# Seven block products for the SwiGLU input product, on a normalized input, and an output projection by token quarters

## The chip, the cores and the metric

The kernel runs on one core of a Trainium2 chip. The metric is the device time of one execution in microseconds (us). A run lists one time for each of several executions, and their median counts.

## The reference

One step of a one-layer hybrid decoder, in float32, on 1024 prompt tokens and 8 decode tokens (T = 1032 columns), model width 1024. The part in front (a mixer of three sliding-window attention groups and a Mamba-2 branch) is the same in both kernels. The change begins where its two results are projected back:

```python
mix = concatenate([attn, ssm]) @ w_out          # 512 + 1024 features -> 1024
h = x + rmsnorm(mix, norm_mix_post)
hcat = rmsnorm(h, norm_ffn_pre) @ w_ffn_in      # 1024 -> 2 x 2816
gate, up = hcat[..., :2816], hcat[..., 2816:]
y = h + rmsnorm((silu(gate) * up) @ w_ffn_out, norm_ffn_post)
```

## The kernel before

Features lie on the 128 partitions and tokens in the columns. Every large product is made exact to float32 in three passes: each operand is split into a high part in float32r and the rest, and a `unit` issues, for each of its k tiles, high x high, low x high and high x low into one PSUM bank (line 169). The tokens go in three chunks of 344 columns (`CH`). Weights come in tiles of 1024 columns through two `wr` buffers; `load_w` splits them into `wh` and `wl`, two buffers each, mostly on GpSimd (lines 156 and 158).

The order of instructions on each engine is fixed when the program is built: a planner takes the ready instruction with the lowest priority number, and the block `prio(kind)` around code gives the number: "evac" comes first, then "w" (weights), "side", and "main" (the large products) last. A tile of a pool takes a slot (`bufs`) when the last reader of an earlier tile is done with it. All transfers are issued from SyncE's queue (SP). `next_copy` spreads the copies of the decode caches (88 of about 1 MB each) over the large products at `RATE` copies for each evacuated unit.

**Output projection** (lines 937 to 1040). The state-space part of the first two chunks is multiplied for all eight tiles m into `mix[m]`, then the attention part for chunk 0 and chunk 1, and, ahead of chunk 2, its state-space part. For each chunk a column sum of squares is built from `acc` and `sq` (`stat`), `finish` sums it over the partitions with a matmul of ones and takes the root and the reciprocal (`rms`, line 192), and then the chunk is normalized, the residual is added, and the result is written to DRAM (`h_d`) and split into `fh` and `fl`, scaled by the next norm's weights alone. The row scale `rf` of that norm is applied after the SwiGLU product. `fh` and `fl` take the 16 slots of the pool `act` that `sh` and `sl`, the split state-space input, held.

**SwiGLU** (lines 1042 to 1180). Hidden tiles t = 0 to 21 are taken in four groups (6, 6, 6 and 4 tiles). `ffn_in` makes for each tile and chunk a unit for the gate (`pg`) and one for the up half (`pu`), 24 matmuls of 344 columns each; VectorE and ScalarE turn them into silu(gate) x up, split into `hh` and `hl`, which stay on chip. After each group `ffn_out` multiplies its tiles with their rows of `w_ffn_out` and adds the result to `fac`. The first two tiles' last chunk is put late, so that other chunks cover its norms. The last group works in chunks of 388, 388 and 256 columns (`CL`), with its weights `ow` split ahead and the residual `hres` loaded back from `h_d`; after each chunk comes the last norm, and the output is added and stored.

## Time and profile before

| | us |
|---|---|
| median of 3 runs | 1949.28 |
| lowest and highest run | 1946.99, 1952.03 |
| the profiled execution: its span, first to last instruction (no other time of it is listed) | 1955.3 |
| TensorE matmul busy | 1827.1 (93%) |
| VectorE busy | 1071.0 (55%) |
| GpSimd busy | 856.4 (44%) |
| ScalarE busy | 549.2 (28%) |

The span is that of one profiled execution, 6.0 us above the median of the runs. Busy shares are averages over stages with different limits, so windows of single stages are read instead. PE is TensorE's matmul, PEld its weight load, DVE is VectorE, ACT is ScalarE, POOL is GpSimd, SP is SyncE; us from the span's start place a row. Matmuls are pipelined and their recorded lengths overlap, so the pace is read from their starts.

### The profile page before, as it was taken

To read this page: it belongs to the slowest core of one execution; us is meant where nothing else is said; L and a number is where in the kernel's file an instruction comes from. 1 tells how busy PE (TensorE), PEld (TensorE's weight loads), DVE (VectorE), ACT (ScalarE), POOL (GpSimd) and SP (SyncE) were. 2 spreads that over 40 slices of the span, in tenths; PEclk is the share of its full clock that TensorE was granted. 3 is DMA by queue.
4 is the path that set the end of the run, shared out by engine and by line. 5 is a ranking of instruction groups with operands and counts; after the bars stand their busy time and mean duration, and the time that the engine had idled before them with its cause. 6 is when DMAs were issued, how large, how long until landed. Compare 5 with 4: busy or idle time off the path is not lost.

```text
span 1955.3 us, 29265 instructions
## 1 busy us (share of the span) xinstructions
PE 1827.1 (93%) x11685; PEld 1712.4 (88%) x11685; DVE 1071.0 (55%) x1917; ACT 549.2 (28%) x1084; POOL 856.4 (44%) x557
## 2 busy tenths in 40 slices
PE   7999989999999999998789889999999999999994
PEld 7998777888887898886678879999999999999993
DVE  7866776768774554556884796330233223321348
ACT  5322344343533344452231334111111001100142
POOL 6332356665435534356755564223223332233325
PEclk9999999999999999999889999999999999999997
DMA  5322333443324433365554444236533753355362
GB/s 188 114 92 87 111 110 100 126 127 110 117 83 153 161 99 104 130 233 150 154 158 130 134 134 151 97 128 244 178 108 103 253 172 119 119 202 196 116 251 87
DMA packets 125545, 275.27 MB, mean 141 GB/s; under 512 B 17616, under 2 KB 83632, under 8 KB 124000
## 3 DMA queue, kind: packets, MB, share of 16 engines
q1 hardware_dynamic: 125408, 273.39, 42.8%
q8 instruction: 92, 1.51, 0.3%
q14 instruction: 45, 0.37, 0.1%
HBM read 235.86 MB, written 125.47 MB: 185 GB/s over the span
## 4 chain that ended last, share of the span: by engine, by line
PE 39%; DVE 7%; DMA 2%; issue 1%; POOL 1%; ACT 1%; DVEq 0%; SPq 0%; POOLq 0%; ACTq 0%
PE g L169 14%; PE pu L169 12%; PE pg L169 12%; DMA nt<-n_d 1%; DVE mix L1030 1%; DVE fl L1033 1%; PE g L954 1%; DVE nt L856 1%; DVE nt L855 1%; DMA xr<-in_xT 0%; DVE mix L1029 0%; POOL nt L854 0%; DVE fr L192 0%; DVE nr L192 0%; DVE sl L924 0%
## 5 line engine op out<-in xcount | busy, mean ns | idle before, releaser
L169 PE MATMUL g<-xh,wh 128*128 128x344 f32 x1344 | 446.0, 332 | 32.4 <-DVE rw L239 12.7
L169 PE MATMUL g<-xl,wh 128*128 128x344 f32 x1344 | 443.2, 330 | 2.8 <-DVE xl L218 2.7
L169 PE MATMUL g<-xh,wl 128*128 128x344 f32 x1344 | 441.9, 329 | 1.9 <-POOL wl L158 1.2
L156 POOL TENSOR_SCALAR wh<-wr 128x1024 fp32r<-128x1024 f32 (+1 forms) x133 | 140.4, 1056 | 674.5 <-PE g L169 355.8
L158 POOL TENSOR_TENSOR wl<-wr,wh 128x1024 fp32r<-128x1024 f32 (+1 forms) x133 | 312.8, 2352 | 9.8
L169 PEld LDWEIGHTS g<-xh,wh 128*128 128x128 f32 x1344 | 258.1, 192 | 46.4 <-issue 14.4
L169 PEld LDWEIGHTS g<-xh,wl 128*128 128x128 f32 x1344 | 258.1, 192 | 11.5 <-issue 7.5
L169 PEld LDWEIGHTS g<-xl,wh 128*128 128x128 f32 x1344 | 258.0, 192 | 11.0 <-issue 6.1
L239 DVE TENSOR_TENSOR u<-pu,rf 128x344 f32<-128x344 f32 x66 | 34.0, 515 | 237.5 <-PE pu L169 237.5
L169 PE MATMUL pg<-fh,wh 128*128 128x344 f32 x504 | 158.8, 323 | 4.9 <-DVE mix L1010 4.9
L169 PE MATMUL pg<-fl,wh 128*128 128x344 f32 x504 | 162.1, 322 | 0.0
L169 PE MATMUL pu<-fl,wh 128*128 128x344 f32 x504 | 161.8, 321 | 0.0
L169 PE MATMUL pg<-fh,wl 128*128 128x344 f32 x504 | 161.4, 320 | 0.0
L169 PE MATMUL pu<-fh,wh 128*128 128x344 f32 x504 | 161.0, 319 | 0.0
L169 PE MATMUL pu<-fh,wl 128*128 128x344 f32 x504 | 160.4, 318 | 0.0
L169 PE MATMUL g<-hl,wh 128*128 128x344 f32 x432 | 137.8, 319 | 0.0
L169 PE MATMUL g<-hh,wl 128*128 128x344 f32 x432 | 137.4, 318 | 0.0
L169 PE MATMUL g<-hh,wh 128*128 128x344 f32 x432 | 137.1, 320 | 0.0
L659 ACT ACTIVATE sm<-sm,ngm 128x128 f32<-128x128 f32 (+1 forms) x192 | 84.9, 443 | 183.5 <-DVE ngm L655 177.2
L1088 ACT CAST hh<-s 128x344 fp32r<-128x344 f32 x66 | 31.7, 480 | 296.6 <-DVE s L1087 296.6
L614 ACT COPY sw<-rw 32x1032 f32<-32x1032 f32 x96 | 101.0, 1052 | 30.5 <-DVE rw L239 29.4
L1085 ACT ACTIVATE s<-s 128x344 f32<-128x344 f32 x66 | 32.5, 492 | 247.6 <-DVE s L239 247.4
(325 smaller groups left out, 3815.9 us busy)
## 6 DMA issues: line engine op xcount, KB each, us to landing
out_skv<-in_cache SPq DMA_DIRECT2D x64, 1023.5 KB, 5.4
wr<-in_w_in SPq DMA_DIRECT2D x56, 512.0 KB, 3.7
wr<-in_w_fin SPq DMA_DIRECT2D x44, 512.0 KB, 3.6
out_skv<-in_cache SPq DMA_DIRECT2D x16, 1022.0 KB, 5.4
wr<-in_w_out SPq DMA_DIRECT2D x24, 512.0 KB, 4.7
wr<-in_w_fout SPq DMA_DIRECT2D x24, 384.0 KB, 3.9
e<-cs_d SPq DMA_DIRECT2D x16, 512.0 KB, 4.1
n_d<-nh SPq DMA_DIRECT2D x12, 512.0 KB, 3.6
```

What stands on the lines that cost most here:

```text
L156: nc.gpsimd.tensor_scalar(out=wh[:, :cols], in0=wr[:, :cols], scalar1=1.0, scalar2=0.0, op0=ALU.mult, op1=ALU.add)
L158: nc.gpsimd.tensor_tensor(out=wl[:, :cols], in0=wr[:, :cols], in1=wh[:, :cols], op=ALU.subtract)
L169: nc.tensor.matmul(ps, x[:, ws], y[:, c0:c1], start=(k == 0 and j == 0), stop=(k == n - 1 and j == 2))
L239: return nc.vector.tensor_tensor(out=dst, in0=ps, in1=r[:dst.shape[0], c0:c1], op=ALU.mult)
L614: nc.scalar.copy(sw[q * 32:(q + 1) * 32, 0:T], rw[s * 32:(s + 1) * 32, :])
L659: nc.scalar.activation(out=sm[:, h, :nk], in_=sm[:, h, :nk], func=AF.Exp, scale=SCALE, bias=ngm[:, g, j, i:i + 1], accum_out=den[:, g, j, ...
L855: nc.vector.tensor_tensor(out=nt[:, 0], in0=nt[:, 0], in1=nt[:, 1], op=ALU.add)
L856: nc.vector.tensor_tensor(out=nt[:, 0], in0=nt[:, 0], in1=nt[:, 2], op=ALU.add)
L954: nc.tensor.matmul(pq[m][c], ws[m][j == 1][:, k * P:(k + 1) * P], (sl if j == 2 else sh)[k][:, CH[c][0]:CH[c][1]], start=(k == 0 and j == ...
L1030: nc.vector.scalar_tensor_tensor(out=mv, in0=mv, scalar=nw(MIX_POST, m), in1=x[:, m % 2], op0=ALU.mult, op1=ALU.add)
L1085: last = nc.scalar.activation(out=s, in_=s, func=AF.Silu)
L1088: nc.scalar.copy(hh[:, c0:c1], s)
```

## The change

The tokens go in four quarters of 258 columns (`QS`) from the output projection on, and the tiles `mix[q][i]` hold one quarter and four of the eight feature tiles, 4 x 258 columns.

**Output projection.** The state-space part is made for quarters 0 to 2, then the attention part for quarters 0 and 1 together, for quarter 2, the state-space part of quarter 3 and its attention part. The attention weights are loaded and split again for each of the three attention parts (12 pairs; before 8, with two pairs kept on chip). `norms(q)` normalizes, adds the residual in the tile that held x (`xr`, three buffers, two for a quarter), writes it to `h_d`, and makes the second norm before the SwiGLU product: its reciprocal is applied to the input itself.

**SwiGLU input product.** Two token halves s, each of two quarters. The weights of gate and up of one hidden tile, and the input of one half, are each cut into 2 x 2 blocks. `x_blocks(s)` forms from the four input blocks seven combinations (b11, b21, b22, t1 to t4) in place, with five subtractions of 1032 columns, and splits each into high and low (ScalarE copies; the rest on VectorE for four, on GpSimd for three). `w_blocks(t)` does the same for the weights with four sums of 512 columns and seven splits. `ffn_in(t, s, w)` makes seven products of 4 x 3 matmuls of 258 columns, each in a PSUM bank of its own out of eight, and adds them to the two quarters of gate and up. The product silu(gate) x up goes to DRAM (`hid_d`), not to the chip's own memory.

**Output product.** It begins when all 22 hidden tiles are made. `hid_load(t)` reads a tile back through an `xr` buffer and splits it into two slots out of 28 (16 of the pool `act`, 12 of `ax`), which the x blocks held before. `ffn_out` is as before, but the weights `ow` and the residual tiles `hres` of the last group take `act` slots after those of the hidden tiles. `RATE` for the copies falls from 0.52 to 0.42 for each call of `next_copy`, of which there are two in each `ffn_in`.

The core of the diff (empty lines and removed code left out):

```diff
+QW = T // 4
+QS = [(i * QW, (i + 1) * QW) for i in range(4)]
+RATE = (0.35, 0.42)
...
+    mix = [[mixp.tile([P, 4, QW], F32, tag="mix", name=f"mix{q}{i}") for i in range(2)] for q in range(4)]
+    def mv(q, m):
+        return mix[q][m // 4][:, m % 4]
+    def ssm_ev(m, ps, a0, a1):
...
+    C3 = [(0, 388), (388, 3 * QW)]
+    pq = [[gps(cw=y - x) for x, y in C3] for m in range(2)]
...
+    def ssm_part(ms, qs, share=False):
+        for m in ms:
+            w = ssm_w(m, share)
+            for q in qs:
+                ps = gps(cw=QW)
+                unit(ps, w, sh, sl, q, QS)
+                with prio("evac"):
+                    next_copy(ssm_ev(m, ps, *QS[q]))
+    ssm_part(range(2, KT), (0, 1, 2))
...
+    def att_part(qs):
+        accs = {q: np_.tile([P, QW], F32, tag="nacc", name="nacc") for q in qs}
+        for m in range(KT):
+            if m % 2 == 0:
+                pair = load_pair(m)
+            for q in qs:
+                ps = gps(cw=QW)
+                unit(ps, [x[:, (m % 2) * 512:(m % 2 + 1) * 512] for x in pair], ahs, als, q, QS)
+                with prio("evac"):
+                    nc.vector.tensor_tensor(out=mv(q, m), in0=mv(q, m), in1=ps, op=ALU.add)
+                    stat(mv(q, m), m == 0, accs[q], nc.vector)
+        return accs
...
+    def norms(q, acc):
+        c0, c1 = QS[q]
+        with prio("evac"):
+            r = np_.tile([P, QW], F32, tag="nr", name="nr")
+            finish(acc, r)
+            acc = np_.tile([P, QW], F32, tag="nacc", name="nacc2")
+            hs = []
+            for i in range(2):
+                x = np_.tile([P, 4, QW], F32, tag="xr", name="xr", bufs=3)
+                nc.sync.dma_start(out=x, in_=a["xT"][4 * i:4 * i + 4, :, c0:c1].rearrange("k p t -> p k t"))
+                hs.append(x)
             for m in range(KT):
+                h = hs[m // 4][:, m % 4]
+                (nc.gpsimd if m % 2 else nc.vector).tensor_tensor(out=mv(q, m), in0=mv(q, m), in1=r, op=ALU.mult)
+                nc.vector.scalar_tensor_tensor(out=h, in0=mv(q, m), scalar=nw(MIX_POST, m), in1=h, op0=ALU.mult,
+                                               op1=ALU.add)
+                stat(h, m == 0, acc, nc.gpsimd)
+            r = np_.tile([P, QW], F32, tag="nr", name="nr2")
+            finish(acc, r)
+            for m in range(KT):
+                nc.vector.scalar_tensor_tensor(out=mv(q, m), in0=hs[m // 4][:, m % 4], scalar=nw(FFN_PRE, m), in1=r,
+                                               op0=ALU.mult, op1=ALU.mult)
+            for i in range(2):
+                nc.sync.dma_start(out=h_d[i][:, :, c0:c1].rearrange("k p t -> p k t"), in_=hs[i])
+    acc01 = att_part((0, 1))
+    norms(0, acc01[0])
+    norms(1, acc01[1])
+    norms(2, att_part((2,))[2])
+    ssm_part(range(KT), (3,), True)
+    norms(3, att_part((3,))[3])
...
+    ax = pool(fst, "ax", 12, side="right")
+    ex = pool(fst, "ex", 2, side="right")
+    slots = [(actp, "act")] * 16 + [(ax, "ax")] * 12
+    half = {}
+    def x_blocks(s):
+        (xa, xc), (xb, xd) = mix[2 * s], mix[2 * s + 1]
+        def split(name, x, e):
+            p, tag = slots.pop(0)
+            hi = p.tile([P, T], F32R, tag=tag, name=f"x{name}h{s}")
+            p, tag = slots.pop(0)
+            lo = p.tile([P, T], F32R, tag=tag, name=f"x{name}l{s}")
+            xf = x.rearrange("p k t -> p (k t)")
+            nc.scalar.copy(hi, xf)
+            e.tensor_tensor(out=lo, in0=xf, in1=hi, op=ALU.subtract)
+            half[s, name] = (hi, lo)
+        def sub(dst, x, y):
+            nc.vector.tensor_tensor(out=dst, in0=x, in1=y, op=ALU.subtract)
         with prio("evac"):
+            split("b11", xa, nc.vector)
+            sub(xa, xb, xa)
+            split("b21", xc, nc.gpsimd)
+            split("b22", xd, nc.gpsimd)
+            sub(xb, xd, xb)
+            sub(xd, xd, xa)
+            split("t2", xd, nc.vector)
+            split("t1", xa, nc.vector)
+            split("t3", xb, nc.gpsimd)
+            sub(xc, xc, xd)
+            split("t4", xc, nc.vector)
+    x_blocks(0)
+    x_blocks(1)
+    hid_d = [dtile(f"hid_d{t}", [P, T]) for t in range(HT)]
+    wslots = [(whp, "wh"), (wlp, "wl"), (whp, "wh"), (wlp, "wl"), (ex, "ex"), (ex, "ex")] + [(mixp, "mix")] * 8
+    nws = [0]
+    banks = [(psg, "g"), (psa, "ap"), (pss, "sp"), (pst, "ap"), (psg, "g"), (psa, "ap"), (pss, "sp"), (psn, "ap")]
...
+    def w_blocks(t):
+        res = {}
+        with prio("w"):
+            g = wrp.tile([P, 1024], F32, tag="wr", name="wg")
+            nc.sync.dma_start(out=g, in_=a["w_fin"][t])
+            u = wrp.tile([P, 1024], F32, tag="wr", name="wu")
+            nc.sync.dma_start(out=u, in_=a["w_fin"][HT + t])
+            sa = rowp.tile([P, T], F32, tag="row", name="sa")
+            sb = rowp.tile([P, T], F32, tag="row", name="sb")
+            a11, a12, a21, a22 = g[:, :512], g[:, 512:], u[:, :512], u[:, 512:]
+            s1, s2, s3, s4 = sa[:, :512], sa[:, 512:1024], sb[:, :512], sb[:, 512:1024]
+            def split(name, x):
+                p, tag = wslots[nws[0] % len(wslots)]
+                nws[0] += 1
+                w = p.tile([P, 1024 if p in (whp, wlp) else T], F32R, tag=tag, name=f"w{name}")
+                nc.scalar.copy(w[:, :512], x)
+                nc.gpsimd.tensor_tensor(out=w[:, 512:1024], in0=x, in1=w[:, :512], op=ALU.subtract)
+                res[name] = w
+            split("b11", a11)
+            nc.vector.tensor_tensor(out=s1, in0=a21, in1=a22, op=ALU.add)
+            split("b21", a12)
+            nc.vector.tensor_tensor(out=s2, in0=s1, in1=a11, op=ALU.subtract)
+            split("t2", s2)
+            split("t1", s1)
+            nc.vector.tensor_tensor(out=s3, in0=a11, in1=a21, op=ALU.subtract)
+            split("t3", s3)
+            nc.vector.tensor_tensor(out=s4, in0=a12, in1=s2, op=ALU.subtract)
+            split("b22", s4)
+            split("t4", a22)
+        return res
+    def ffn_in(t, s, w):
+        def prod(name):
+            q, tag = banks[nbk[0] % 8]
+            nbk[0] += 1
+            ps = q.tile([P, 512], F32, tag=tag, name="fb")[:, :QW]
+            wt, (hi, lo) = w[name], half[s, name]
+            with prio("main"):
+                for k in range(4):
+                    wh, wl = wt[:, k * P:(k + 1) * P], wt[:, 512 + k * P:512 + (k + 1) * P]
+                    xk = slice(k * QW, (k + 1) * QW)
+                    for j, (x, y) in enumerate(((wh, hi), (wl, hi), (wh, lo))):
+                        nc.tensor.matmul(ps, x, y[:, xk], start=(k == 0 and j == 0), stop=(k == 3 and j == 2))
+            return ps
+        p = np_.tile([P, 4, QW], F32, tag="xr", name="fp", bufs=3)
+        o_ = np_.tile([P, 4, QW], F32, tag="xr", name="fo", bufs=3)
+        p1, u2, p5, u3 = (p[:, i] for i in range(4))
+        gate, up = o_[:, 0:2], o_[:, 2:4]
+        def add(dst, x, y, e=nc.vector):
+            return e.tensor_tensor(out=dst, in0=x, in1=y, op=ALU.add)
+        b = prod("b11")
+        with prio("evac"):
+            nc.scalar.copy(p1, b)
+        b = prod("b21")
+        with prio("evac"):
+            next_copy(add(gate[:, 0], p1, b))
+        b = prod("t2")
+        with prio("evac"):
+            add(u2, p1, b)
+        b = prod("t1")
+        with prio("evac"):
+            nc.scalar.copy(p5, b)
+            add(gate[:, 1], u2, p5)
+        b = prod("t3")
+        with prio("evac"):
+            add(u3, u2, b)
+            add(up[:, 1], u3, p5)
+        b = prod("b22")
+        with prio("evac"):
+            add(gate[:, 1], gate[:, 1], b)
+            nc.scalar.activation(out=gate, in_=gate, func=AF.Silu)
+        b = prod("t4")
+        with prio("evac"):
+            next_copy(add(up[:, 0], u3, b))
+            nc.vector.tensor_tensor(out=up, in0=up, in1=gate, op=ALU.mult)
+            nc.sync.dma_start(out=hid_d[t][:, 2 * s * QW:(2 * s + 2) * QW], in_=up.rearrange("p i t -> p (i t)"))
...
+    hslots = [(actp, "act")] * 16 + [(ax, "ax")] * 12
+    nhs = [0]
+    def hid_load(t):
+        with prio("w"):
+            hr = np_.tile([P, T], F32, tag="xr", name="hr", bufs=3)
+            nc.sync.dma_start(out=hr, in_=hid_d[t])
+            res = []
+            for i in range(2):
+                p, tag = hslots[nhs[0] % 28]
+                nhs[0] += 1
+                res.append(p.tile([P, T], F32R, tag=tag, name=f"h{'hl'[i]}{t}"))
+            nc.scalar.copy(res[0], hr)
+            (nc.vector if t % 2 else nc.gpsimd).tensor_tensor(out=res[1], in0=hr, in1=res[0], op=ALU.subtract)
+        hid[t] = res
...
-                nc.sync.dma_start(out=h, in_=h_d[m])
+                nc.sync.dma_start(out=h, in_=h_d[m // 4][m % 4])
...
+    for t in range(HT):
+        w = w_blocks(t)
+        for s in range(2):
+            ffn_in(t, s, w)
+    fac = [mixp.tile([P, T], F32, tag="mix", name=f"fac{m}") for m in range(KT)]
     for gi, (t0, t1) in enumerate(groups):
-        if gi == 0:
-            # the last chunk of the first two tiles late, while its norms are under way
-            ffn_in((0, 1), [(0, 0), (0, 1), (1, 0), (1, 1), (0, 2), (1, 2)])
-        for t in range(2 if gi == 0 else t0, t1):
-            ffn_in((t,), [(t, c) for c in range(3)])
+        for t in range(t0, t1):
+            hid_load(t)
```

## Rows read from the trace of the kernel before

**Rows 1.** Windows in order: length, busy us (instructions) by engine, granted clock, DMA share, GB/s.

```profile
991.90:1069.00 77.10, 69.09 (x381) 66.53 (x382) 46.00 (x52) 11.55 (x19) 43.08 (x23) 0.90 0.48 142
1069.00:1098.00 29.00, 29.00 (x185) 28.78 (x184) 21.50 (x29) 8.96 (x15) 11.60 (x7) 1.00 0.23 72
1098.00:1172.00 74.00, 57.59 (x320) 54.26 (x320) 64.62 (x72) 27.67 (x54) 48.34 (x32) 0.93 0.51 162
1172.00:1201.00 29.00, 25.24 (x155) 24.43 (x153) 23.95 (x34) 16.27 (x28) 17.14 (x13) 0.96 0.53 180
1201.00:1877.00 676.00, 676.00 (x4291) 675.85 (x4290) 189.21 (x301) 76.57 (x157) 207.03 (x130) 1.00 0.45 153
1930.00:1955.30 25.30, 1.22 (x2) 0.50 (x2) 18.12 (x22) 2.32 (x5) 14.96 (x14) 0.55 0.30 105
```

**Rows 2.** The chain that ended last: start, length, work.

```profile
1312.05 67.74 PE g L169 x432
...
1877.56 23.36 PE g L169 x132
```

**Rows 3.** Timeline of TensorE, last output group: start, length of the merged instructions.

```profile
1919.13 0.80 PE L169 MATMUL g<-hh,ow 128*128 128x256 f32 x2 [4.15 <-DVE fac L1132]
...
1924.45 0.40 PE L169 MATMUL g<-hh,ow 128*128 128x256 f32 x2
...
1926.91 0.40 PE L169 MATMUL g<-hh,ow 128*128 128x256 f32 x2
```

**Rows 4.** Costs by line, GpSimd and ScalarE, from 990 us on: busy, mean ns.

```profile
L1119 POOL TENSOR_TENSOR ow<-wr,ow 128x512 fp32r<-128x512 f32 x8 | 11.0, 1410 | 19.7 <-ACT ow L1118 19.7
...
L979 POOL TENSOR_TENSOR wl<-wr,wh 128x1024 fp32r<-128x1024 f32 x6 | 14.5, 2424 | 15.0 <-ACT wh L978 15.0
...
L1118 ACT CAST ow<-wr 128x512 fp32r<-128x512 f32 x8 | 4.6, 617 | 3.7 <-PE pu L169 2.4 <-DMA wr<-in_w_fout 1.2
```

**Rows 5.** Costs by line on VectorE, 1069 to 1201 us.

```profile
L1033 DVE SCALAR_TENSOR_TENSOR fl<-mix,par,fh 128x344 fp32r<-128x344 f32 x24 | 23.2, 1001 | 1.1 <-ACT fh L1032 1.0
L1030 DVE SCALAR_TENSOR_TENSOR mix<-mix,par,xr 128x344 f32<-128x344 f32 x24 | 21.9, 952 | 2.2 <-DMA xr<-in_xT 2.2
L995 DVE TENSOR_TENSOR nacc<-nacc,sq 128x344 f32<-128x344 f32 x21 | 17.5, 835 | 6.7 <-ACT sq L994 5.9
L1029 DVE TENSOR_TENSOR mix<-mix,nr 128x344 f32<-128x344 f32 x12 | 13.3, 1170 | 0.1
L1010 DVE TENSOR_TENSOR mix<-mix,g 128x344 f32<-128x344 f32 x24 | 11.8, 500 | 2.9 <-PE g L169 2.9
...
L154 DVE TENSOR_TENSOR wl<-wr,wh 128x1024 fp32r<-128x1024 f32 x4 | 5.4, 1358 | 0.0
```

**Rows 6.** VectorE: costs from 990 us on, one tile's row (ns min/median/max), timeline.

```profile
L924 DVE SCALAR_TENSOR_TENSOR sl<-yg,par,sh 128x1032 fp32r<-128x1032 f32 x5 | 8.5, 1707 | 0.0
...
L1132 DVE TENSOR_TENSOR fac<-fac,g 128x256 f32<-128x256 f32 x8 | 3.2, 412 | 0.3 <-PE g L169 0.3
...
L192 DVE RECIPROCAL fr<-fr 128x256 f32<-128x256 f32 x1 | 1.8, 1753 | 1.9 <-ACT fr L191 1.9
...
L1167 DVE TENSOR_TENSOR fac<-fac,hres x5: 410/411/943, 1947.4 to 1949.8; 128x256 f32<-128x256 f32 x5
...
984.51 2.83 DVE L924 SCALAR_TENSOR_TENSOR sl<-yg,par,sh 128x1032 fp32r<-128x1032 f32 x1
...
992.11 1.28 DVE L924 SCALAR_TENSOR_TENSOR sl<-yg,par,sh 128x1032 fp32r<-128x1032 f32 x1
```

**Rows 7.** DMA issues: count, KB each, median us to landing.

```profile
wr<-in_w_fin SPq DMA_DIRECT2D x44, 512.0 KB, 3.6
...
hres<-h_d SPq DMA_DIRECT2D x8, 516.0 KB, 10.0
```

**Rows 8.** The tail: cost by line on GpSimd, and the chain.

```profile
L1161 POOL TENSOR_TENSOR fac<-fac,hres 128x388 f32<-128x388 f32 x9 | 11.4, 1293 | 0.0
...
1941.84 1.76 DVE fr L192
```

130 lines of the change are left out of this document (25 added, 105 removed).

## The prediction

> **What bounds the kernel now.** I read the windows first, cut where the engines' shares change [rows 1]. From 1201 to 1877 us TensorE is busy for all 676.00 us at full clock, while VectorE needs 189, GpSimd 207 and ScalarE 77: hidden tiles (into SwiGLU) and their output products alternate and only matmuls set the pace. Ahead of it, between 1098 and 1201, the reader is to see the reverse: VectorE is busy 64.6 of 74.0 and 24.0 of 29.0 us, TensorE only 57.6 and 25.2. That is the seam, where the output projection, two norms and the first hidden tiles meet. Behind 1930 a tail of 25.3 us has almost no matmul. So the change has three prices, each from its own stretch: matmuls in the full stretch, VectorE in the seam, transfers at the two new joints behind it.
>
> Then the pace of one matmul. The chain of waits has 432 matmuls of 344 columns in 67.74 us, 156.8 ns each [rows 2]. At 256 columns, 21 matmuls start between 1924.45 and 1926.91 us, 117.1 ns each [rows 3]; so 258 columns are 118.0 ns, and the matmul costs by column (0.456 and 0.457 ns each).
>
> **The SwiGLU product.** Before: 22 tiles x 3 chunks x 2 halves x 24 = 3168 matmuls x 156.8 = 496.7 us. After: 22 tiles x 2 token halves x 7 products x 12 = 3696 x 118.0 = 436.1 us. That is -60.6 us, or 19.8 us a tile. It holds only if nothing else needs 19.8 us. POOL splits seven 512-column blocks, 1.41 us each [rows 4]: 9.9 us, where it now has two of 1024 columns. ScalarE copies them (7 x 0.62, [rows 4]) and has six short passes, some 7 us. VectorE: ten adds from PSUM at 0.41, four between SBUF tiles and two products of 516 columns, four sums of 512: with the doubling that POOL causes (below) about 12.5 us. All are under 19.8, and eight PSUM banks let an evacuation be some 10 us late. So the saving is taken in full.
>
> A page speaks against it. In the Trainium skill, "TensorE: Matmul & The Clock Gate", section "Back-to-back issue gap", a stream of weight loads and matmuls is said to run at about 81 ns for 128 columns and 131 ns for 512. An estimate between these gives 98 ns at 258 and 109 at 344, and the product would get 17 us slower (3696 x 98 against 3168 x 109), the sum below 2016 us of span. Here the rows decide: 117 against 157 ns [rows 2, 3].
>
> **The seam.** The output projection's matmuls keep their columns (96 of 387 columns, 177 ns by column, and 1008 x 118 ns are 135.9 us, against 864 x 156.8 = 135.5), so what counts is who feeds them. State-space parts and attention for quarters 0 and 1 are 90.7 us of matmul. In the same stretch now, 106.1 us hold 566 matmuls, some 14 of them small [rows 1]: 552 x 156.8 = 86.6, so 19.5 us are lost. The same loss puts their end at 991.9 + 90.7 + 19.5 = 1102.
>
> From there VectorE has to do, before the last of the x blocks is split: the other two quarters' evacuations, 16 x 0.41 + 14 x 0.63 = 15.4 us; the norms, per quarter 4 products (0.88), 8 residuals (0.71), 8 scalings (0.75) and two reciprocals of 1.75, 18.7 us, four times 74.8; the state-space part of quarter 3, 8 x 0.41 + 4 x 1.36 = 8.7; x_blocks, 2 x 9 operations on 1032 columns at 1.70 = 30.6; first evacuations and weight sums, 7. In all 136.5 us. The prices are the means of the seam [rows 5], those of 344 columns times 258/344, and for the wide ones the scaled split of the same width [rows 6]. Now the whole seam from 1069 to 1201 has 110.1 us of VectorE work [rows 1]; x_blocks is the part that is new. It can't move forward: its tiles take the slots of sh and sl, which the state-space part of quarter 3 reads to its end, and it ends with a chain: norm, second norm, three differences, splits.
>
> The means are uncertain, and here lies the range. A two-input operation from SBUF takes 0.41 us alone and 0.94 beside one of POOL at 256 columns; at 1032 columns the rows have 1.28 and 2.83 [rows 6]. An add from PSUM stays at 0.50 [rows 5]. The Trainium skill, "SBUF — State Buffer", section "Who interferes with whom", says that a VectorE instruction with two SBUF inputs contends with a GpSimd one that reads SBUF; by that rule, which the trace bears out, x_blocks pays for its own splits on POOL. Of the 136.5 us, 94 such narrow operations (4 x 20 and 14) and 18 wide ones are 100; the rest, 36.3, is fixed. All alone, 36.3 + 94 x 0.41 + 18 x 1.28 = 98 us; all contended, 36.3 + 94 x 0.94 + 18 x 2.83 = 176. I take 130, nearer to the means: norms, weight splits and x_blocks keep POOL busy as now, but in the last 30 us it has only splits, so eight scalings and nine wide operations cost 6 us less.
>
> So the last block is ready at 1102 + 130 = 1232. By then TensorE has had all of tile 0 but the last product (1.4 us), and up to three products of tile 1 (4.2 us), whose weights find slots. The product thus behaves as if it had begun at 1232 + 1.4 - 19.8 - 4.2 = 1209.9. Before, counted back from 1877.56, it behaves as if it began at 1877.56 - 496.7 - 3 x 67.74 = 1177.7 [rows 2]. The seam costs +32 us (0 to +77 with the bounds).
>
> **Joint into the output product.** The hidden tiles come back from DRAM into three xr buffers that the last two ffn_in calls still hold. Only tile 0 can be loaded early; five loads follow, two or three at a time, each 3.6 to 10.0 us [rows 7], with a split of about 1.1 us on ScalarE and 1.36 on VectorE or 2.4 us on POOL behind it [rows 4, 5]. A wave of loads and splits takes some 7 us, and the sixth tile comes with the second, 14 us after the last product. Meanwhile the six free banks can take tile after tile, 18 matmuls or 2.8 us each. No overlap costs 12 us, full overlap 3; I take 7, with the matmuls at half clock behind a wait: the two behind the 4.15 us one took 0.80 us in place of 0.40 [rows 3].
>
> **Joint into the last group.** Its weights (ow) take act slots that group 2 reads until its end, so the first split (0.62 + 1.41 us, [rows 4]) is bare: +3 us (1 to 5). Now they are split while hidden tiles run.
>
> **The tail.** hres needs eight act slots. Now fh and fl are done with them in time; after the change tiles 18 to 21 sit there and the last unit reads them. The eight loads, 10.0 us to landing each when queued together [rows 7], move behind the last matmul, and with them 16 adds of 388 columns (nine of them on POOL, 1.29 us each, [rows 8]). The last norm's reciprocal already ends at 1943.6 [rows 8], 14 us after the last matmul, with VectorE busy 18.1 of the tail's 25.3 us [rows 1]; the adds fall in beside it and leave VectorE freer ahead of it. Nine adds on POOL, 11.6 us, from 12 us on, when hres has landed, end some 24 us behind the last matmul, and a store follows: +2 us (-4 to +12). Slower pacing (0.42 in place of 0.52) leaves some eight cache copies for the last group in place of four; they are issued ahead of hres, at nothing, and if they delay it, within that +12.
>
> **Sum.** 1955.3 - 60.6 + 32 + 7 + 3 + 2 = 1938.7 us for the span. The profiled span is 6.0 us above the median of the runs, 1949.28; the same distance gives 1933 us. A measurement here can tell 0.3%, 5.8 us, from no change.
>
> **Rivals.** (a) The seam stays hidden: VectorE's operations run as if alone, no loss, 1906.7, a time of 1901. For it: POOL is busy for only 0.65 of 1098 to 1172 us. Against it: the means, measured at that share, are 1.5 to 2 times the least values. (b) It ends slower: the seam takes the gain. That decides once VectorE's 130 us become 147 (+48.6 us, the net gain without the seam). The x_blocks splits and 12 pair splits (2.4 us) on POOL raise its share, and a contended mean half way between 136 and 175 puts the seam at +58: 1964, a time of 1958. For it: windows that are already 87% VectorE. Against it: list order puts the attention's evacuations into gaps. (c) The full stretch isn't TensorE's any more: in-order evacuations on VectorE behind contended sums cost 1 us a tile, +22 us, time 1955. For it: VectorE's share rises from 0.28 to 0.63; against: 10 us of banks. (d) The change doesn't do what it says: a matmul of 258 columns costs as 344. 3696 x 156.8 = 579.5 us, +143 against the sum, 2076. The page above points this way; the 256-column rows speak against it.
>
> **How the numbers follow.** Forecast 0.48 (its own range 1918 to 1950), (a) 0.17, (b) 0.25, (c) 0.08, (d) 0.02. The range for 8 in 10 reaches from (a) into (b): 1902 to 1967. Chances, by the same cases. Faster: 0.42 of the forecast, (a) whole, 0.01 of (c): 0.60. Within 0.3% (1943.4 to 1955.1): 0.05 and 0.04 and 0.04 of forecast, (b) and (c): 0.13. Slower: the rest, 0.27.
>
> **What would show it.** Right: seven products of 12 matmuls at 118 ns without idle time between tiles, 436 us; a VectorE busy over 0.85 from 1100 to 1230; first steady tile at about 1232; a gap under 10 us ahead of the first output unit; hres landing behind the last matmul. Wrong: waits of TensorE on POOL or VectorE inside the 22 tiles, a seam that ends before 1215 or after 1250, or a joint with a bare 15 us.

## The result, and the profile after

The kernel after takes 1972.9 us (median of four runs, 1971.74 to 1975.82), the one before 1949.65 (four runs, 1946.99 to 1952.03): a ratio of 1.0120, 95% interval 1.0105 to 1.0136. It is slower by 1.2%, where the forecast was 1933 us and its range ended at 1967. The profiled execution took 1973.6 us, with a span of 1971.8.

Windows of the kernel after, columns as in [rows 1]:

```profile
1069.00:1098.00 29.00, 28.09 (x234) 27.83 (x232) 18.81 (x31) 12.56 (x23) 11.45 (x5) 1.00 0.23 73
1098.00:1130.00 32.00, 22.54 (x149) 20.98 (x150) 26.47 (x32) 7.97 (x14) 22.03 (x19) 0.88 0.41 132
1130.00:1155.00 25.00, 19.17 (x113) 18.54 (x113) 17.34 (x25) 7.57 (x14) 17.64 (x16) 0.77 0.63 190
1155.00:1180.00 25.00, 18.77 (x114) 17.78 (x113) 22.95 (x30) 8.10 (x15) 17.16 (x8) 0.83 0.42 127
1180.00:1217.00 37.00, 13.49 (x58) 10.90 (x57) 32.19 (x31) 14.75 (x29) 27.88 (x21) 0.60 0.21 71
1217.00:1252.00 35.00, 16.27 (x76) 14.34 (x76) 29.40 (x45) 11.23 (x20) 16.56 (x15) 0.64 0.24 76
1252.00:1679.00 427.00, 426.57 (x3562) 426.53 (x3563) 230.01 (x428) 142.34 (x275) 208.40 (x148) 1.00 0.51 169
...
1930.00:1972.00 42.00, 9.50 (x69) 8.31 (x67) 29.16 (x38) 8.55 (x20) 21.81 (x20) 0.64 0.68 258
```

The full stretch is what was forecast: TensorE busy for all of 427 us at full clock (2.4 GHz), the other engines at half load. The loss is ahead of it. From 1180 to 1252 TensorE is busy for 29.8 of 72 us, at a granted clock of 0.60 to 0.64, and VectorE, the engine that was to set this stretch, has 10.4 us of idle time in it too.

The chain that ended last, its longest pieces from 1240 us on (start, length, work); it answers to [rows 2, 8]:

```profile
1252.43 427.00 PE fb L1152 x3564
1680.23 6.02 DMA hr<-hid_d
1687.44 4.15 DMA hr<-hid_d
1698.12 216.06 PE g L171 x1354
...
1928.97 7.27 DMA hres<-h_d
1937.17 2.49 DVE fr L194
```

3564 matmuls in 427.00 us are 119.8 ns each. The product thus counts 3696 x 119.8 = 442.8 us, and, ending at 1679.4, behaves as if begun at 1236.6. The first matmul of the last group stands at 1890.7 and its last one ends at 1938.3 (1877.4 and 1929.9 before). The terms, against the profile before:

| term | forecast | measured | from |
|---|---|---|---|
| SwiGLU product | -60.6 | -53.9 | 442.8 - 496.7 |
| seam | +32 | +58.9 | 1236.6 - 1177.7 |
| joint into the output product | +7 | +8.1 | 1890.7 - 1679.4 - 3 x 67.74 |
| last group | +3 | -4.9 | 47.6 - 52.5 |
| tail | +2 | +8.1 | 33.5 - 25.4 |
| sum | -16.6 | +16.3 | spans: 1971.8 - 1955.3 = 16.5 |

Four fifths of the miss (26.9 of 33.1 us of span) are the seam; it is the term that turned the sign. These positions are counted from the span's start, and the part ahead of the change, which both kernels share, was 4.7 us shorter in this profile than in that of the kernel before: its last two splits of the state-space input start at 996.34 us before (first row) and at 991.61 us after (second row).

```profile
996.34 2.48 DVE L924 SCALAR_TENSOR_TENSOR sl<-yg,par,sh 128x1032 fp32r<-128x1032 f32 x2
991.61 2.49 DVE L926 SCALAR_TENSOR_TENSOR sl<-yg,par,sh 128x1032 fp32r<-128x1032 f32 x2
```

Counted from their ends (998.82 and 994.10), the seam costs 242.5 - 178.9 = 63.6 us.

VectorE's reciprocals mark its steps: two for each norm, one row per instruction (x2: two back to back). The first row is norm 0's first, the second norm 0's second and norm 1's first, then norm 1's second, and norm 2's and 3's pairs:

```profile
1099.35 1.75 DVE L194 RECIPROCAL nr<-nr 128x258 f32<-128x258 f32 x1
...
1121.99 3.38 DVE L194 RECIPROCAL nr<-nr 128x258 f32<-128x258 f32 x2
...
1165.70 1.75 DVE L194 RECIPROCAL nr<-nr 128x258 f32<-128x258 f32 x1
...
1174.77 1.75 DVE L194 RECIPROCAL nr<-nr 128x258 f32<-128x258 f32 x1
...
1215.51 1.76 DVE L194 RECIPROCAL nr<-nr 128x258 f32<-128x258 f32 x1
...
1222.90 1.77 DVE L194 RECIPROCAL nr<-nr 128x258 f32<-128x258 f32 x1 [0.69 <-ACT nr L193]
...
1239.33 1.77 DVE L194 RECIPROCAL nr<-nr 128x258 f32<-128x258 f32 x1 [4.84 <-ACT nr L193]
```

The start at 1099 is the forecast's 1102. But norms 1 and 2 need 42 and 41 us from one reciprocal to the next, 83 of the 160 us up to the last x block (1259.8). The kernel before has such a norm too, with 41.6 us between the reciprocals of its chunk 1, but its second reciprocal (`rf`) is applied behind the product, which therefore does not wait for it:

```profile
1125.26 2.29 DVE L192 RECIPROCAL nr<-nr 128x344 f32<-128x344 f32 x1
...
1166.85 2.29 DVE L192 RECIPROCAL rf<-rf 128x344 f32<-128x344 f32 x1
```

GpSimd's timeline inside norm 2 of the kernel after shows what stands in between (L1012 are the seven adds of its second sum, L1125 splits of SwiGLU weights, L1080 one of an x block):

```profile
1190.61 1.89 POOL L1012 TENSOR_TENSOR nacc<-nacc,sq 128x258 f32<-128x258 f32 x2 [2.46 <-ACT sq L1011]
1192.45 2.54 POOL L1080 TENSOR_TENSOR xt3l<-mix,xt3h 128x1032 fp32r<-128x1032 f32 x1
1194.96 2.28 POOL L1125 TENSOR_TENSOR wt<-sa,wt 128x512 fp32r<-128x512 f32 x1
1197.18 1.73 POOL L1012 TENSOR_TENSOR nacc<-nacc,sq 128x258 f32<-128x258 f32 x1
1199.05 2.09 POOL L1125 TENSOR_TENSOR wt<-wu,wt 128x512 fp32r<-128x512 f32 x1
1202.42 1.54 POOL L1125 TENSOR_TENSOR wb<-sb,wb 128x512 fp32r<-128x512 f32 x1 [1.28 <-ACT wb L1124]
1203.92 0.73 POOL L1012 TENSOR_TENSOR nacc<-nacc,sq 128x258 f32<-128x258 f32 x1
1205.86 2.95 POOL L1125 TENSOR_TENSOR wb<-wg,wb 128x512 fp32r<-128x512 f32 x2 [1.21 <-ACT wb L1124]
1208.77 2.31 POOL L1012 TENSOR_TENSOR nacc<-nacc,sq 128x258 f32<-128x258 f32 x2
1211.27 1.48 POOL L1125 TENSOR_TENSOR wt<-sa,wt 128x512 fp32r<-128x512 f32 x1 [0.19 <-ACT wt L1124]
1212.71 0.91 POOL L1012 TENSOR_TENSOR nacc<-nacc,sq 128x258 f32<-128x258 f32 x1
```

The adds are spread over 23 us, and splits of SwiGLU weights, some of them waiting for ScalarE, stand between them. The order of GpSimd's list is not the only cause: there are two buffers for squares, and the last three squares came at 1202.25, 1206.21 and 1211.10 us, behind weight copies in ScalarE's list, though VectorE had their inputs ready at 1192.8 (with more buffers, in e17 below, they come at once). TensorE's own waits show the same from the other side (1095 to 1256 us; us in total, times, longest):

```profile
PE nps L1003 <- POOL nacc L1012: 18.2, 2, 11.2
PE fb L1152 <- ACT xt1h L1079: 7.7, 1, 7.7
```

The ones-matmul that finishes a norm waits at the head of TensorE's list, and what stands behind it waits as well. That is 18.2 of the 63.7 us in which TensorE has no matmul between 1099.35 and 1259.8 us.

### The profile page after: what moved, and what is told of

Same layout as the page of the kernel before. It is cut to its first block, busy times and chain, and to the rows that moved or that the text cites. A ratio compares the mean times of both kernels' runs of the same rounds, so it can differ in the third digit from the quotient of the medians.

```text
span 1971.8 us, 31805 instructions
## 1 busy us (share of the span) xinstructions
PE 1791.5 (91%) x12457; PEld 1673.1 (85%) x12457; DVE 1184.3 (60%) x2167; ACT 655.4 (33%) x1266; POOL 974.6 (49%) x657
## 4 chain that ended last, share of the span: by engine, by line
PE 36%; DVE 9%; DMA 3%; issue 1%; ACT 1%; POOL 1%; DVEq 0%; POOLq 0%; SPq 0%; ACTq 0%
PE fb L1152 22%; PE g L171 14%; DMA nt<-n_d 1%; DVE nacc L1012 1%; DVE mix L1048 1%; DVE xr L1042 1%; PE g L968 1%; DVE fac L1277 1%; DVE nr L194 1%; DMA hr<-hid_d 1%; DVE mix L1084 1%; DVE mix L1041 0%; DVE al L860 0%; DMA hres<-h_d 0%; ACT wh L996 0%
## 5 line engine op out<-in xcount | busy, mean ns | idle before, releaser
L158 POOL TENSOR_SCALAR wh<-wr 128x1024 fp32r<-128x1024 f32 (+1 forms) x91 | 96.7, 1062 | 322.6 <-PE g L171 298.3
L160 POOL TENSOR_TENSOR wl<-wr,wh 128x1024 fp32r<-128x1024 f32 (+1 forms) x91 | 210.9, 2317 | 6.8 <-PE fb L1152 0.8
L1125 POOL TENSOR_TENSOR wb<-wg,wb 128x512 fp32r<-128x512 f32 x44 | 58.4, 1349 | 167.6 <-ACT wb L1124 167.6
L171 PEld LDWEIGHTS g<-hh,wh 128*128 128x128 f32 x432 | 81.5, 189 | 5.4 <-ACT hh L1205 5.0
L617 POOL TENSOR_TENSOR sw<-sw,sin 128x1032 f32<-128x1032 f32 x24 | 71.4, 2975 | 21.8 <-ACT sw L616 21.8
L171 PEld LDWEIGHTS g<-hl,wh 128*128 128x128 f32 x432 | 81.1, 189 | 1.1 <-POOL hl L1206 1.1
L1161 DVE TENSOR_TENSOR fo<-fp 128x258 f32<-128x258 f32 x88 | 58.8, 668 | 38.4 <-ACT fp L1174 37.0
L171 PEld LDWEIGHTS g<-hh,wl 128*128 128x128 f32 x432 | 81.6, 189 | 0.0
L241 DVE TENSOR_TENSOR rw<-g,rin 128x344 f32<-128x344 f32 x108 | 54.7, 510 | 39.1 <-PE g L171 38.9
L653 DVE CUSTOM_DVE_ANT_0 sm<-sps,mask 128x128 f32<-128x128 f32 (+1 forms) x192 | 59.0, 345 | 27.5 <-PE ptp L668 17.3
```

The source lines that it names most:

```text
L158: nc.gpsimd.tensor_scalar(out=wh[:, :cols], in0=wr[:, :cols], scalar1=1.0, scalar2=0.0, op0=ALU.mult, op1=ALU.add)
L160: nc.gpsimd.tensor_tensor(out=wl[:, :cols], in0=wr[:, :cols], in1=wh[:, :cols], op=ALU.subtract)
L171: nc.tensor.matmul(ps, x[:, ws], y[:, c0:c1], start=(k == 0 and j == 0), stop=(k == n - 1 and j == 2))
L241: return nc.vector.tensor_tensor(out=dst, in0=ps, in1=r[:dst.shape[0], c0:c1], op=ALU.mult)
L617: nc.gpsimd.tensor_tensor(out=sw[:, 0:T], in0=sw[:, 0:T], in1=sin, op=ALU.mult)
L653: nc.vector.tensor_tensor_reduce(out=sm[:, h, :nk], in0=sps[h][:, c0:c0 + nk], in1=msk, scale=1.0, scalar=0.0, op0=ALU.add, op1=ALU.max, a ...
```

## The experiments

Ratios are to the kernel before, run on the same chip; "gain" is the difference to 1.0120 times 1949 us. The intervals are 3 to 6 us to either side and that of 1.0120 itself is 3, so a gain under 5 us is none that this can tell, and the 6 us of e7 and e14 are only just clear of it. Where a seam's length is compared below, it is counted from the end of the shared part (the last split of `sl`) to the point at which the product behaves as if begun: 242.5 us in the kernel after, 240.3 in e13, which is the same kernel up to its last store.

| run | edit | ratio | 95% interval | gain, us |
|---|---|---|---|---|
| e1 | own ring of three for the norms' x | 1.0124 | 1.0100 to 1.0148 | -1 |
| e2 | four squares, six sums | 1.0105 | 1.0081 to 1.0129 | 3 |
| e3 | sums of squares on TensorE, three squares | 1.0025 | 1.0007 to 1.0042 | 18.5 |
| e4 | second sums on VectorE | 1.0114 | 1.0092 to 1.0135 | 1 |
| e5 | order in pairs of quarters | 1.0053 | 1.0032 to 1.0074 | 13 |
| e6 | second norm left out | 0.9990 | 0.9976 to 1.0004 | 25 |
| e7 | x differences left out | 1.0087 | 1.0069 to 1.0104 | 6 |
| e8 | early residual tiles | 1.0079 | 1.0058 to 1.0100 | 8 |
| e9 | e3, e5, e8 | 0.9964 | 0.9947 to 0.9981 | 30 |
| e10 | e9, hidden tiles into row tiles | 0.9933 | 0.9916 to 0.9949 | 36 |
| e11 | e10, attention 2 and 3 together | 0.9930 | 0.9910 to 0.9951 | 37 |
| e14 | scaling in wide instructions | 1.0153 | 1.0134 to 1.0172 | -6 |
| e15 | e11, hidden tiles into row and ex | 0.9920 | 0.9901 to 0.9939 | 39 |
| e16 | e15 and e14 | 0.9935 | 0.9916 to 0.9953 | 36 |
| e17 | separate rings of squares | 1.0117 | 1.0085 to 1.0148 | 1 |
| e18 | e15, separate rings of squares | 0.9899 | 0.9884 to 0.9914 | 43 |

**Are the rings of buffers the wait? (e1, e2, e17)**

```diff
-  x = np_.tile([P, 4, QW], F32, tag="xr", name="xr", bufs=3)
+  x = nrm.tile([P, 4, QW], F32, tag="hs", name="xr", bufs=3)     # e1
+  sq = nrm.tile(..., tag="sq", bufs=4); nacc: bufs=6             # e2
+  sq = nrm.tile(..., tag="sq" if eng is nc.gpsimd else "sqa", bufs=4); nacc: bufs=6   # e17
```

> Three theories of the seam, used for all runs on it. From the first norm's first reciprocal (1098.7 us) to the last x block (1259) VectorE is busy 134 of 160 us; the forecast had 130 and no idle time. Rings: the norms queue for few buffers (two squares, two sums, three xr tiles, which the SwiGLU sums fp and fo share), and VectorE's 26 us of idle time come from that. Work: VectorE's 134 us set the end, and a wait that is taken away only lets other work move up. Queues: the sums of squares of the norms stand on GpSimd between weight splits (the third norm's seven adds took from 1190.6 to 1212.7, with less than 1 us each), and TensorE's ones-matmul behind them holds TensorE as well. This run gives the norms' x tiles a ring of three of their own; fp, fo and hr keep the old one. Rings: 6 to 12 us faster (1961 to 1967), with tile 0's first sums in VectorE before the last norm's scaling. Work and queues: within 3 us of 1973.

> Four squares in place of two and six sums in place of two. Rings: the statistics of quarter 2, whose evacuations end at 1116 but whose adds come at 1155 behind the second norm's squares, move up by some 30 us, and the time falls by 8 to 15 us (1958 to 1965). Work and queues: within 3 us of 1973.

> The squares of the attention parts (added up on VectorE) and those of the norms' second sums (added up on GpSimd) get rings of four of their own, so that the first sums of quarters 2 and 3 can't stand behind the second sums of quarters 1 and 2 for a buffer, and six sum tiles. Rings, in the form that the shared ring leaves the first sums waiting even at four buffers: 8 to 15 us faster (1956 to 1963), with the first reciprocal of quarter 2 before 1150 us. Queues (one gate behind the next: ScalarE's and GpSimd's order holds the second sums wherever the first ones stand): within 4 us, with the third norm's two reciprocals 40 us or more apart.

Not by themselves. In e1 the SwiGLU sums did move ahead (the first stands at 1188.12 in place of 1245.80), and the time stayed. In e17 quarter 2's first reciprocal came with norm 1's second, both at 1162 (1174.77 after), not before 1150, and its second one at 1201.99, 38 us later. In e17 the adds of that norm are no longer spread: with four squares the same seven adds take 10.7 us in place of 23:

```profile
1182.10 5.21 POOL L1014 TENSOR_TENSOR nacc<-nacc,sq 128x258 f32<-128x258 f32 x5 [4.15 <-ACT nacc L1009]
...
1189.89 2.86 POOL L1014 TENSOR_TENSOR nacc<-nacc,sq 128x258 f32<-128x258 f32 x2
```

ScalarE takes the root at 1195.28, and then VectorE comes to the reciprocal only at 1201.99, behind adds and x splits in its own list:

```profile
1195.78 2.58 DVE L1014 TENSOR_TENSOR nacc<-nacc,sq 128x258 f32<-128x258 f32 x1
1198.28 1.22 DVE L1082 TENSOR_TENSOR xt2l<-mix,xt2h 128x1032 fp32r<-128x1032 f32 x1
1199.42 1.22 DVE L1082 TENSOR_TENSOR xt1l<-mix,xt1h 128x1032 fp32r<-128x1032 f32 x1
1200.57 1.50 DVE L1014 TENSOR_TENSOR nacc<-nacc,sq 128x258 f32<-128x258 f32 x1
1201.99 1.75 DVE L194 RECIPROCAL nr<-nr 128x258 f32<-128x258 f32 x1
```

The seam is 242.3 us long in e1, 237.1 in e2 and 237.7 in e17: buffers are worth some 5 us of it at most. In e2 VectorE was busy 143.5 of 155.5 us between the first reciprocal and the last block, where it had 134.1 of 160.3 (idle time in the kernel after: 26.2): half of the idle time was filled, and most of what filled it was the same instructions taking longer.

**VectorE's work, GpSimd's work, or the order of the lists? (e3, e4, e7, e14)**

```diff
-  eng.tensor_tensor(out=acc, in0=acc, in1=sq, op=ALU.add)
+  nc.tensor.matmul(ps[:, :QW], onr, sq, start=(m == 0), stop=(m == KT - 1))   # e3, sq in fp32r, bufs=3
-  stat(h, m == 0, acc, nc.gpsimd)
+  stat(h, m == 0, acc, nc.vector)                                             # e4
-  nc.vector.tensor_tensor(out=dst, in0=x, in1=y, op=ALU.subtract)             # e7: sub() does nothing
-  for m in range(KT): nc.vector.scalar_tensor_tensor(out=mv(q, m), in0=h, scalar=nw(FFN_PRE, m), in1=r, ...)
+  nc.scalar.activation(out=mv(q, m), in_=h, func=AF.Copy, scale=nw(FFN_PRE, m))        # e14, behind stat
+  for i in range(2): nc.vector.tensor_tensor(out=mix[q][i], in0=mix[q][i], in1=r..., op=ALU.mult)
```

> The sums of squares leave VectorE and GpSimd: the squares are written as fp32r and TensorE adds them up in PSUM, 64 matmuls with ones of 258 columns (0.12 us each at full clock, 8 us in all) for 56 adds. That takes some 22 us from GpSimd and 15 from VectorE in this stretch. Work: 12 to 18 us faster (1955 to 1961). Queues: 15 to 25 us faster (1948 to 1958), with the third norm's two reciprocals under 25 us apart where they were 41. Rings: at most 5 us faster, since the rings of x tiles and the list order stay.

> The norms' 28 second sums move from GpSimd to VectorE, 0.43 to 0.8 us each, 12 to 22 us more for VectorE. Work: 8 to 20 us slower (1981 to 1993). Queues: 5 to 12 us faster (1961 to 1968), since no norm's end stands behind a weight split any more. Rings: within 4 us.

> The eight differences of the x blocks are left out (the blocks are split as they are): 13.0 us of VectorE, five of them ahead of the last block. Work: 8 to 14 us faster (1957 to 1963). Queues and rings: the first half's four stand beside waits anyway, so only the second half's four count, 3 to 6 us faster (1965 to 1968).

> The FFN norm's weights are multiplied in by ScalarE while the second sum is still being added up, and VectorE then scales by the row in two instructions of 1032 columns (1.23 us each alone) in place of eight of 258 (19.5 us for 32 in the kernel after). That takes 8 to 12 us of work from VectorE and 3 us from each norm's chain; ScalarE gets 32 passes of 0.42 us. Work or pair: 6 to 10 us faster (1963 to 1967). Queues: the norms' waits for the sums stay, only the last norm's 2 to 3 us count, at most 4 us faster.

Taking the adds from both engines gained 18 us, the upper end for work and the middle for queues; the third norm's reciprocals stand 21 us apart (1161.65 and 1182.75). As e3 also has a third buffer for squares, its gain is that of both. Handing GpSimd's adds to VectorE changed the time by 1 us, which neither forecast (the seam of that profile is 236.5 us long): VectorE was busy 143.3 of 155.5 us, GpSimd 82 in place of 104. Leaving out 13 us of VectorE's differences gave back 6, the queues' end. And e14 took 32 narrow products (19.5 us) off VectorE for eight wide ones (10.3 us) and was slower by 6: ScalarE went from 56 to 69 us busy between the first reciprocal and the last block, with 32 more passes in its list, and the last norm's second reciprocal came behind a longer wait (4.84 us in the kernel after):

```profile
1243.62 1.77 DVE L194 RECIPROCAL nr<-nr 128x258 f32<-128x258 f32 x1 [6.64 <-ACT nr L193]
```

So VectorE's work alone does not set the seam: less of it brought no gain in e14.

**What do the two engines cost each other? (e13)**

```diff
+  for i in range(16): v(nd[:, 0], nx[:, 0], nr_[:, 0])      # VectorE, 258 columns, alone
+  for i in range(16): g(np1[:, 0], np1[:, 0], nd[:, 0])     # GpSimd alone
+  for i in range(32): v(nd[:, 1], nx[:, 1], np1[:, 0])      # VectorE beside
+  for i in range(16): g(np2[:, 0], np2[:, 0], np1[:, 0])    # GpSimd
   ...                                                       # and 1032 columns: 8 and 8 alone, 4 alone, 8 beside 4
```

> The kernel after with a small block of its own behind the last store, so that only the block's rows count, not the time: VectorE products of 258 columns alone, GpSimd adds of 258 alone, then 32 of the one beside 16 of the other; then the same with differences of 1032 columns, 8 alone, 4 on GpSimd alone, 8 beside 4. If the two engines share one thing in turn (pair): beside GpSimd a VectorE product takes 0.8 us or more where it takes 0.47 alone, and the stretch of both is near the sum of the two alone (15 and 12 us: 23 to 27 us). If they only disturb each other at times (work): under 18 us for both.

Timeline of that block, a row for a run of like instructions (GpSimd's two stretches run on into each other, so each row holds the one alone and the one beside VectorE):

```profile
1978.14 8.22 DVE L1313 SCALAR_TENSOR_TENSOR mb<-mb,par,mb 128x258 f32<-128x258 f32 x16
1986.49 26.70 POOL L1316 TENSOR_TENSOR mb<-mb,mb 128x258 f32<-128x258 f32 x32 [16.61 <-DVE mb L1313]
1999.35 22.48 DVE L1313 SCALAR_TENSOR_TENSOR mb<-mb,par,mb 128x258 f32<-128x258 f32 x32 [12.99 <-POOL mb L1316]
...
2032.79 10.10 DVE L1330 TENSOR_TENSOR mb<-mb,mb 128x1032 f32<-128x1032 f32 x8
2042.96 23.05 POOL L1316 TENSOR_TENSOR mb<-mb,mb 128x1032 f32<-128x1032 f32 x8 [20.35 <-DVE mb L1330]
2052.66 18.25 DVE L1334 TENSOR_TENSOR mb<-mb,mb 128x1032 f32<-128x1032 f32 x8 [9.77 <-POOL mb L1316]
```

A narrow product alone takes 8.22 / 16 = 0.51 us. GpSimd's first 16 adds end at about 1999.3 (0.80 each), the other 16 at 2013.2. Of the 32 products, 16 ran beside these, from 1999.35 to 2013.5 (0.88 each), and 16 alone up to 2021.8. Beside each other the two go in step, one product and one add every 0.87 us. The whole stretch of 22.5 us lies between what the two theories gave (under 18, and 23 to 27). The wide difference takes 1.26 us alone and the wide add 2.4; together, from 2052.7 to 2066.0, four adds and four differences took 3.3 us each. The two engines thus nearly take turns on wide tiles (both together need 90% of the sum of the two alone) and do less so on narrow ones (67%). The Trainium skill, "SBUF — State Buffer", section "Who interferes with whom", calls the shared port pair an exclusive lock: the wide rows nearly agree, the narrow ones only in part. So 16 adds on GpSimd cost the 16 products beside them 5.9 us (14.1 in place of 8.2), 0.37 us an add, and the shortest such add on VectorE takes 0.36. This is a part of why e4 came out even, not the whole: VectorE's busy time there still rose by 9 us (143.3 for 134.1), and its idle time fell from 26 to 12.

**The start of the seam and the second norm (e5, e6)**

```diff
-  C3 = [(0, 388), (388, 3 * QW)];  ssm_part(range(2, KT), (0, 1, 2))
+  C3 = QS[:2];                     ssm_part(range(2, KT), (0, 1))              # e5
-  norms(2, att_part((2,))[2]);  ssm_part(range(KT), (3,), True)
+  ssm_part(range(KT), (2, 3), True);  norms(2, att_part((2,))[2])
-  stat(h, m == 0, acc, nc.gpsimd);  r = np_.tile(..., name="nr2");  finish(acc, r)   # e6
```

> Nothing but the order of the output projection changes: the state-space part of quarters 0 and 1, their attention part and norms, then the state-space part of quarters 2 and 3, and so on. 192 matmuls of 258 columns (22.7 us) move from ahead of the first norm to behind it, with as many loads and splits as now. Work (VectorE's sum with its start): the first reciprocal comes 20 to 23 us earlier, at about 1077 us, and the time falls by 12 to 20 us (1951 to 1959). Queues and rings: the norms start earlier but meet twice the weight splits and matmuls in the same queues, and the last x block moves by under 8 us, 1963 to 1971.

> The second norm is left out: the x blocks are scaled by the first norm's row in place of the second's. That removes 32 squares, 28 adds on GpSimd, four ones-matmuls and four reciprocals (7 us of VectorE), and the wait for them; the 32 scalings stay. It prices what the seven products need ahead of them and the kernel before had behind its product. Queues: these waits are the seam's idle time, 25 to 35 us faster (1936 to 1946). Work: 7 us of VectorE and what the 22 us of adds on GpSimd cost its neighbours, 10 to 18 us faster (1953 to 1961).

In e5 the first reciprocal came at 1085.1 (forecast 1077), 14 us earlier (16 counted from the end of the shared part), and 13 us reached the end. Without the second norm the time is that of the kernel before. That is what a product on normalized input costs here: between the first reciprocal and the last block VectorE is busy for 126.9 of 134.9 us in place of 134.1 of 160.3, so 7 us of work and 18 us of idle time went. How much of these waits is due to GpSimd's adds is not separated.

**Tail, joint, and the kernel before again (e8, e12, e9 to e11, e15, e16, e18)**

```diff
-  h = actp.tile([P, T], F32, tag="act", name=f"hres{m}")
+  h = ax.tile([P, T], F32, tag="ax", name=f"hres{m}")                      # e8
-  hr = np_.tile([P, T], F32, tag="xr", name="hr", bufs=3)
+  hr = (rowp.tile(tag="row") if t % 2 == 0 else np_.tile(tag="xr"))       # e10
+  hr = (rowp.tile(tag="row") if t % 2 else ex.tile(tag="ex"))             # e15
-  norms(2, att_part((2,))[2]);  norms(3, att_part((3,))[3])
+  acc23 = att_part((2, 3));  norms(2, acc23[2]);  norms(3, acc23[3])      # e11, e15, e16, e18
+  sq = nrm.tile([P, QW], F32R, tag=tag, bufs=4)     # e18: tag "sqa" for attention parts, "sq" for norms
```

> The residual tiles of the tail take slots that are free from group 2's loads on, in place of those that the last unit reads. The tail from the last matmul to the end was 33.5 us, 25.3 before. If hres sets it: back to 25 to 27 us, 6 to 9 us faster (1962 to 1965). If VectorE sets it (adds, products and two reciprocals behind each other): at most 3 us faster. If the hres loads, now early, delay the weights of the last group behind them: slower.

In e8 the tail is back at 25.2 us, but the last group takes 51.9 us in place of 47.6 (52.5 before): the 16 residual adds and their products, on GpSimd and VectorE, stand either in the last group or in the tail. The span fell by 4.4 us; the ratio says 8, with 4 to either side.

> The kernel before, profiled a second time. The forecast took 6.0 us from its sum because the profiled span, 1955.3 us, lay that far above the median of the runs; the kernel after has a span 1.8 us under its own time. If the first profile was of a slow execution: a span of 1943 to 1950 us, and a place in it that is 5 to 10 us shorter. If spans of this kernel lie above its times: 1953 to 1957 again.

The second profile of the kernel before has a span of 1947.2 us and a time of 1949.0. Its chain, against the same rows of [rows 2]:

```profile
1303.86 67.74 PE g L169 x432
...
1869.37 23.36 PE g L169 x132
```

Both lie 8.2 us earlier. Most of that is older than the seam, as the last splits of the shared part show, at 991.31 us in place of 996.34:

```profile
991.31 2.48 DVE L924 SCALAR_TENSOR_TENSOR sl<-yg,par,sh 128x1032 fp32r<-128x1032 f32 x2
```

So the first profile was 5.0 us late ahead of the change, and its seam was 3.2 us longer than that of the second.

> Three edits together: the order in pairs of quarters (alone 13 us), sums of squares on TensorE (alone 18 us) and early residual tiles (alone 8 us). If they take different terms, they add up: 39 us, a ratio of 0.992 to the kernel before. If the order and the sums take the same idle time of VectorE, 26 to 30 us together, a ratio of 0.997 to 0.999.

> As the run of the three edits, and every second hidden tile that comes back from DRAM lands in one of the two row tiles, which are free once the last tile's weights are summed, in place of the ring of three that the last SwiGLU sums hold. If loads waiting for that ring make the joint: 3 to 6 us less than the run of the three edits, and the first output matmul waits under 1 us. If the landing time of the transfers makes it: within 1.5 us of it.

> As the run before in this group, but the attention parts of quarters 2 and 3 come together, ahead of the norm of quarter 2. If TensorE's part of quarter 3 comes too late for the last norm (its first reciprocal stood 28 us behind the third norm's second one with the sums on TensorE): 4 to 10 us faster. If VectorE sets the end, the order of its work does not matter: within 3 us.

> As the kernel with the order in pairs, both attention parts together, sums on TensorE and early residual tiles, but the hidden tiles come back into the two row and the two ex tiles, none into the ring that the last SwiGLU sums hold. If that ring made what is left of the joint: 3 to 6 us faster than that kernel, a ratio of 0.990 to 0.992. If the landing of the last tile's own stores or of the loads makes it: within 1.5 us of it, 0.993.

> The run before in this group with the wide scaling as well. If the scaling counts as it does alone: 5 to 10 us less than that run. If the seam is by now TensorE's or the last norm's chain alone: 1 to 4 us less.

> The fastest kernel so far (order in pairs, both attention parts together, sums on TensorE, early residual tiles, hidden tiles into row and ex tiles; 0.992 of the kernel before) with two rings of four squares. If the shared ring of squares still holds quarter 2 and 3's first sums (quarter 2's first reciprocal came at 1170 us, 50 us behind quarter 1's second): 5 to 12 us faster. If the order of the matmuls sets that: within 2 us.

The three edits of e9 give 30 us together, not 39: the order and the sums draw on the same stretch. The row tiles gave 6 more (the joint into the output product fell from 5.2 us in e9 to 1.3 in e10), and e15 has no joint left, as its chain shows:

```profile
1619.92 25.45 PE fb L1157 x212
1645.37 54.70 PE g L171 x348
```

From its last product (1645.4) to the last group (1849.0) it needs 203.6 us, and three groups of matmuls alone are 203.2. e11 had 1.2 us of the joint left (1648.8 to 1853.2), so e15's buffers could gain little, and e11 against e10, e15 against e11, e16 against e15 and e18 against e15 are inside their intervals. The wide scaling gained nothing here either. The versions e15 and e18 beat both kernels: 0.992 and 0.990 of the one before (1930.4 us against 1947.0, and 1928.5 against 1949.4). In e15 the product behaves as if begun at 1645.4 - 442.8 = 1202.6, 34 us earlier than in the kernel after (32 counted from the end of the shared part).

## Why the prediction was wrong

**The full stretch.** Right in mechanism: no wait of TensorE from 1253 to 1679, with VectorE at half load, so rivals (c) and (d) fell. The price was 1.5% too low, 119.8 ns for 118.0, which is 6.7 us. It was scaled by columns from 117.1 ns at 256. A longer run of 256 columns in the last group takes 117.3 ns before and 118.0 after (over 47 and 53 spacings), so the 21 starts that the price was read from were a little short, and 258 columns cost 0.9 to 1.6 ns more than their share. An estimate from the Trainium skill, "TensorE: Matmul & The Clock Gate", section "Back-to-back issue gap", gave 98 at 258 columns; the trace does not agree.

**The seam, the step that failed.** Its start (1102, measured 1099) and its work (130 us, measured 134.1) were right. What failed is "From there VectorE has to do, before the last of the x blocks is split", read as if a sum of work were a time: VectorE was idle for 26.2 of the 160.3 us, the last block came at 1259.8 in place of 1232, and the product began 27 us late (31 us counted from the end of the shared part: 242.5 in place of 1209.9 - 998.8 = 211.1). The list of work also had one difference too many: `x_blocks` has four subtractions a half, not five as the section on the change has it, so 16 wide operations and not 18, which is 3.4 of the 136.5 us. The prediction named "a chain: norm, second norm, three differences, splits", and costed only its VectorE part. Four norms with two sums each go through ScalarE (squares), GpSimd or VectorE (adds), TensorE (ones), ScalarE (root) and VectorE (reciprocal), each time at the place that the engine's list gives them. Rival (b) had the sign and nearly the size (+58), for a VectorE that works longer; measured, it waited.

What is shown: more buffers alone gain at most some 5 us (e1, e2, e17), though with four squares the second sum takes 10.7 us in place of 23 (e17); which of the two engines adds makes no difference that shows (e4, in part by e13); taking the sums off both, with a third square, gives 18 us, the second norm out 25, an earlier start 13. What stays open is the split of the 27 us between lists, buffers and contention. The prices do not add up (39 became 30), and each relief hands the end to the next step, as e14 and e17 show. A list order written by hand, with no weight split ahead of a norm's adds, was not tried, nor four squares together with the adds on VectorE.

**The joints.** Into the output product: 7, measured 8.1, by the mechanism that was named, the ring that the last sums hold (e10, e15). Last group and tail: +3 and +2, measured -4.9 and +8.1. The prediction saw that hres moves behind the last matmul and that the adds fall into the tail, but not that they then leave the last group, where they had cost 4 us; and the tail had less room for them than forecast (+8.1, inside the +12 of its bound). The first `hres` landed at 1936.2, 2 us ahead of the last matmul's end; GpSimd sat idle for 11.1 us and VectorE for 2.7 until such tiles landed. How much of the 8.1 us is this wait and how much VectorE's own chain is not separated. The sum of both, +3 for +5, was nearly right.

**Taking off 6.0 us.** The sum was made against a profile that lay 6 us above the median, and the difference was taken off the end without knowing where it lay. e12 shows where: of 8.2 us between two profiles of the kernel before, 5.0 lie ahead of the change and 3.2 in the seam. The kernel after had a short shared part too (4.7 us less), so in its span of 1971.8 us a seam that was 31 us late hides behind a front that was 5 us early. The part in front could rightly be taken off; the seam could not, as the new one had been built from absolute times.

## What to carry to other kernels

A sum of work on one engine is a lower bound of a stretch, not its length: where a chain crosses several engines with lists in a fixed order, cost each crossing, and ask what stands in each list between two links. Before a formulation that needs its input normalized (or otherwise finished) ahead of a product, price the chain that so comes onto the path: here it took back more than the 54 us saved in matmuls. Where a profiled execution differs from the median, find out in which stretch before taking the difference off a forecast, and match instructions rather than times: this one began ahead of everything that the change touched.

## What was not expected of the hardware

- A matmul of 258 columns cost 119.8 ns, one of 256 between 117.1 [rows 3] and 118.0 (last group of the kernel after), at the same full clock.
- A narrow VectorE product and a narrow GpSimd add go in step, one of each every 0.87 us (0.51 and 0.80 alone), and a GpSimd instruction is slowed by VectorE too: the wide add went from 2.4 to 3.3 us, while VectorE's wide difference went from 1.26 to 3.3.
- Two executions of the kernel before, with the same instructions in the same order on VectorE, differ by 0.1 us at 206 us, by 6.2 at 722, by 5.0 at 996 and by 8.2 at 1304 (second profile of the kernel before).
